# A decoder layer's MLP on one core: turned sums in small buffers, bank copies at other places of a step

## The chip, the cores and the metric

The kernel runs on one core of a Trainium2 chip. The metric is the device time of one execution in microseconds (us); for a program on one core that is the core's own time. The engines that matter here are TensorE (PE in the profile; its weight loads are listed apart as PEld), VectorE (DVE), ScalarE (ACT), GpSimd (POOL, which here only issues DMAs) and SyncE (SP, whose queue carries the loads). Each engine works through its own instructions in order, and semaphores hold an instruction until what it needs is there.

## The reference

One decoder layer on 256 tokens of width 2048, all in float32: an attention branch and a gated convolution branch, merged; an MLP with squared ReLU of width 8192; a gated embedding at the end. The change lies in the MLP and at its border to the last part.

```python
    h = rms_norm(r, g_mlp[i])
    r = r + jnp.square(jax.nn.relu(h @ w_up[i])) @ w_down[i]
    h = rms_norm(r, g_ple[i])
    r = r + jax.nn.sigmoid(h @ w_ple_gate[i]) * (p[i] @ w_ple_proj[i])
```

## The kernel before

**Two parts of every number.** Matmuls take float32 values as a high part, made by ScalarE (`high`, line 135), and a low part, made by VectorE as value minus high part (`low`, line 138). Three matmuls (high by high, high by low, low by high) make one product. So every weight passes ScalarE once and VectorE once before PE uses it.

**Units and items.** The MLP is a loop of 72 steps, `g` = 0 to 71 (line 917). Step `g` has one *unit*: for `g` below 64, 128 columns of `w_up` (result "up"), then eight units of 128 columns of `w_down` ("dn"). PE computes the unit with 15 matmuls of high parts, 16 of low parts and one more (`cols`) into a single PSUM bank; from step 7 on all units share bank 7. ScalarE copies the bank to SBUF (`evacuated`), and the next unit may start in the bank only after this copy.

The other three quarters of `w_down` are multiplied by a Strassen scheme of seven products, in *items* (side, j). An item loads four blocks of weights (`load_pair`), makes sums of them on VectorE, splits all that into high and low parts (`make`, line 717: B11/B22, then B21, then T1/T3, then T2/T4) and, where it is the first item with this j, also the sums of u, S1 to S4 (`sum_u`, split with them). In the step after its `make`, PE multiplies them into seven banks P1 to P7 (`products`, line 776; the order is P1, P3, P5, P7, P2, P6, P4). Most steps have a whole item. Items with j of 24 and more, and two others, are spread over two steps: a *first half-step* (`xs` = 0, 1: B11/B22, the sums of u, T1/T3) and a *second half-step* (`xs` = 2, 3: B21, T2/T4). These are steps 55 to 70.

**Runs and stores.** The seven banks hold the sums of a *run* of items on one side. A run has eight items (the first has four). There are six run ends where the banks have to be given to the other side: `store` (line 793) copies a bank with ScalarE into a tile "part" and issues a DMA on POOL's queue that adds it to DRAM. These 42 copies are queued in `filling`, and `fill()` puts one into ScalarE's order wherever it is called. Before the change all seven are queued at the end of the step in which PE makes the run's last products, so all copies come in the next step: four among the high parts of the next unit and of u, the rest in `make`.

**The stored sums come back.** Late in the loop four `fetch_part` calls (line 807, steps 54, 56, 59 and 61) load stored halves into a tile "raw_p" and queue six jobs each; a step runs two of them behind its bank copy. The first five combine the seven products on ScalarE and VectorE. The last, `turn`, transposes the sums on VectorE into a tile "blocks" and sends them by POOL's queue through DRAM into `r_kept`.

**Buffers.** "slot" is a pool of 44 tiles of 2 KB per partition, from which nearly all small tiles come (u, x, b21, the sums, "part"). Tag "t" has two buffers of 4 KB; "blocks" takes one, and every second item's T2/T4 take two. Tag "raw" has four buffers of 8 KB for weights and "raw_p".

**Order.** From step 2 on `ordered` keeps ScalarE, VectorE, PE and the loads in the order of the program. In one step that order is: `cols` on PE; the parts of the next unit; u of the step before; `make` with the bank's copy in it; two jobs; `products` on PE for the step before. The bank's copy stands behind B11/B22 and the sums of u in a first half-step or a whole step, and behind the high part of T2/T4 in a second half-step (line 766).

**Behind the loop.** In step 71 five of the last inputs x are entered (`enter_high` on ScalarE, `enter_low` on VectorE), P1 is copied twice with a factor each, and sums d and e are made. After the loop come f, c11, the last unit's `dn_done(3, 15)`, the last x, u3, c21, c12 and c22, and PE transposes c11 to c22 between the gate's products.

Of the kernel before, what the change touches and what calls it, by code (L numbers as in the profile page):

```python
# [18 lines left out]
P = 128  # L19
# [19 lines left out]
def hybrid_block_kernel(ctx: ExitStack, tc: tile.TileContext, ins: dict, out: bass.AP):  # L39
# [18 lines left out]
    def slot(shape, dtype, name):  # L58
        return bp.tile(shape, dtype, tag="slot", name=name)
# [75 lines left out]
    def high(hi, src):  # L135
        act(hi, src, AF.Copy)

    def low(lo, src, hi):
        dve.tensor_sub(lo, src, hi.bitcast(F32))
# [577 lines left out]
    def make(a, xs, evacuate):  # L717


        w, j = wS[a], a[1]  # L720
        raw = w["raw"]
        flat = "p a f -> p (a f)"
        fresh = None
        if 0 in xs:
            if j not in sums:
                fresh = sum_u(j)
                sums[j] = tuple(slot([P, 4, P], F32R, f"s_{i}") for i in range(2))
            sh, sl = sums[j]
            for i in range(4):
                w[f"S{i + 1}"] = sh[:, i, :], sl[:, i, :]  # L730
            hi, lo = half_tiles("b")
            keep(w, ("B11", "B22"), hi, lo)
            src = raw[:, 0:2, :].rearrange(flat)
            high(hi, src)
            fill()
            if fresh is not None:
                high(sh, fresh)
            fill()
            low(lo, src, hi)
            fill(len(filling))  # L740
            evacuate()
        if 2 in xs:
            b21 = w["B21"] = tuple(slot([P, CW], F32R, f"b21_{n}") for n in range(2))
            high(b21[0], raw[:, 3, :])
        if 0 in xs:
            dve.tensor_sub(raw[:, 0:3:2, :], raw[:, 0:2, :], raw[:, 2:3, :].to_broadcast([P, 2, CW]))
        if 2 in xs:
            dve.tensor_add(raw[:, 1, :], raw[:, 1, :], raw[:, 0, :])
            low(b21[1], raw[:, 3, :], b21[0])
            dve.tensor_sub(raw[:, 3, :], raw[:, 1, :], raw[:, 3, :])  # L750
        if fresh is not None:
            low(sl, fresh, sh)
        halves = "p (a f) -> p a f"
        if 0 in xs:
            t13 = w["t13"] = half_tiles("t13")
            keep(w, ("T1", "T3"), *t13)
            view = [t.rearrange(halves, a=2) for t in t13]
            high(view[0], raw[:, 0:3:2, :])
            low(view[1], raw[:, 0:3:2, :], view[0])
        if 2 in xs:  # L760
            t24 = half_tiles("t24", items.index(a) % 2 == 0)
            keep(w, ("T2", "T4"), *t24)
            view = [t.rearrange(halves, a=2) for t in t24]
            high(view[0], raw[:, 1:4:2, :])
            if 0 not in xs:
                evacuate()
            low(view[1], raw[:, 1:4:2, :], view[0])


# [37 lines left out]
    def fetch_part(side, h):  # L807
        t = wp.tile([P, 8, S], F32, tag="raw", name="raw_p", bufs=4)
        for i, name in enumerate(ORDER):
            load(t[:, i, :], parts[side, name][:, h * S:(h + 1) * S])  # L810
        p5, p4, p2, p3, p1, p7, p6, z = (t[:, i, :] for i in range(8))
        out = [turned_room(f"turned_s_{side}_{h}_{i}", columns=S) for i in range(2)]

        def first():
            act(z, p1, AF.Copy, scale=up0)
            act(p1, p1, AF.Copy, scale=up1)

        def turn():
            blocks = wp.tile([P, 4, S], F32, tag="t", name="blocks", bufs=2)
            dve.transpose(blocks.rearrange("p a s -> p (a s)"), t[:, 0:4, :].rearrange("p a s -> p (a s)"))  # L820
            for i, half in ((2, 0), (3, 0), (1, 1), (0, 1)):
                nc.gpsimd.dma_start(out[i in (0, 3)][half * P:(half + 1) * P, :], blocks[:, i, :])
            for i in range(2):
                u = 4 * side + 2 * i + h
                st = slot([P, 2, S], F32, "part_in")
                turn_in(st, out[i])
                nc.gpsimd.dma_start(r_kept[u], st, accum_op=ALU.add)

        jobs.extend((
            first,  # L830
            lambda: (scaled(p2, p2, up0, z), scaled(z, p5, down0, z)),
            lambda: (scaled(p3, p3, up0, z), scaled(p7, p7, up1, p1)),
            lambda: (scaled(p7, p6, up1, p7), scaled(p3, p6, up0, p3)),
            lambda: (scaled(p4, p4, down1, p7), scaled(p5, p5, down1, p7)),
            turn,
        ))
# [3 lines left out]
    def fill(n=1):  # L840
        for _ in range(min(n, len(filling))):
            store(*filling.pop(0))
# [74 lines left out]
    for g in range(NU):  # L917
        kind, i = units[g]
        ordered[0] = g > 1
        if g in (5, 7):  # L920
            banks["acc"] = [7, 5] if g == 5 else [7]
        reach = 1 if FIRST <= g < NU - 8 else 2
        for n in range(g + 2, g + reach + 2):
            load_raw(n)
        for a, x in staged[g + 1]:
            if x == 0:
                load_pair(a)
        if g in fetching:
            fetch_part(*fetching[g])
        for u in {NU - 8: (4, 5, 6, 7), NU - 5: (0, 1), NU - 4: (2, 3)}.get(g, ()):  # L930
            load_r(u)
        if g == NU - 3:
            ss2 = slot([P, 2, S], F32, "ss2")
        if g == NU - 2:
            praw = slot([P, 2, S], F32, "p")
            load(praw, ins["pT"].rearrange("p (k s) -> p k s", s=S))
        xs = hT if kind == "up" else {k: uT[16 * i[0] + k] for k in range(16)}
        ps = cols(wU[g][1:], xs, f"{kind}_{g}")
        if g == 0:
            rstd1 = rstd_columns(ss1, "mlp", 1)  # L940
            scales = const.tile([P, 2 * NT], F32, name="scales")
            dve.tensor_mul(scales[:, :NT], rstd1, rstd1)
            dve.tensor_scalar_mul(scales[:, NT:], scales[:, :NT], -1.0)
            up0, up1, down0, down1 = (scales[:, t:t + 1] for t in range(2 * NT))
        if g == 1:
            row1 = rstd_rows(rstd_diag(scales, "mlp"), "mlp")
        done = [n for n in range(g) if n in evac] if g > 1 else []
        ups = [units[n][1] for n in done if units[n][0] == "up"]
        for k in ups:
            up_sum(k, evac.pop(done.pop(0)))  # L950
        halves = []
        while made < g + reach:
            made += 1
            load_raw(made)
            halves += [(made, 0), (made, 1)]
        for h in halves:
            on_act, on_dve = unit_half(*h)
            on_act()
            fill()
            on_dve()  # L960
        for k in ups:
            up_high(k)
        for k in ups:
            up_low(k)
        for n in done:
            dn_done(*units[n][1], evac.pop(n))
        taken = []

        def take():
            if not taken:  # L970
                taken.append(evacuated(ps, kind))

        if staged[g]:
            make(staged[g][0][0], [x for _, x in staged[g]], take)
        fill(len(filling))
        take()
        for _ in range(min(2, len(jobs))):
            jobs.pop(0)()
        entering = {NU - 2: (8, 9), NU - 1: (10, 11, 12, 13, 14)}.get(g, ())
        for n in entering:  # L980
            enter_high(n)
            if n % 2 == 1:
                square(n // 2)
        if g == NU - 1:
            p1 = [evacuated(prod["P1"], "p1", by) for by in (up0, up1)]
        for n in entering:
            enter_low(n)
        if g == NU - 1:
            d, e = (slot([P, CW], F32, n) for n in "de")
            scaled(d, prod["P5"], down0, p1[0])  # L990
            scaled(e, prod["P3"], up0, d)
        evac[g] = taken[0]
        if kind == "up" and i == 63:
            up_sum(i, evac.pop(g))
            up_high(i)
            up_low(i)
        for a, x in staged[g - 1]:
            products(a, x)
            if a in last_of and x == 3:
                filling.extend((a[0], name) for name in NAMES)  # L1000
    assert not jobs


# [36 lines left out]
    f, c11, u3, c12, c21, c22 = (slot([P, CW], F32, n) for n in ("f", "c11", "u3", "c12", "c21", "c22"))  # L1040
    scaled(f, prod["P7"], up1, p1[1])
    scaled(c11, prod["P2"], up0, p1[0])
    dn_done(3, 15, evac.pop(NU - 1))
    enter_high(15)
    square(7)
    scaled(u3, prod["P6"], up1, f)
    scaled(c21, prod["P4"], down1, u3)
    enter_low(15)
    scaled(c12, prod["P6"], up0, e)
    scaled(c22, prod["P5"], down1, u3)  # L1050
# [138 lines left out]
```

## Time and profile before

| | us |
|---|---|
| median of three runs | 1472.6 |
| lowest and highest | 1471.99, 1473.93 |
| profiled execution, its own time | 1475.19 |
| its span, first to last instruction | 1473.4 |
| PE busy | 1428.1 (97%) |
| VectorE busy | 1146.4 (78%) |
| ScalarE busy | 884.2 (60%) |
| POOL busy | 220.7 (15%) |
| mean granted clock of PE | 0.987 |

Shares over the whole span mix stages with different limits. The page's second part, the span in 40 slices, shows where they lie: VectorE is at six or seven tenths up to about 640 us and at nine or more in the MLP's loop; the granted clock is full nearly everywhere, and drops only in stretches from 1200 us on.

The timeline's rows read: start, duration, engine, line, operation, output<-inputs by the program's names, shapes, count, and in brackets how long the engine had been idle before and what released it. Line 87 is the helper for ScalarE, 90 that for PE, 101 that for VectorE, so the names of the tiles tell more than the lines. "w" are the parts of a unit's weights, "raw_s" an item's weights and their sums, "b" those of B11/B22 (wide) or B21 (narrow), "t" those of T1 to T4, "s" those of the sums of u, "a" and "x" u itself, "part" a stored bank, "up" and "dn" the copies of units' banks.

### The profile page before, as it was taken

The numbers are of one execution on the slowest core, as the hardware profiler recorded it, in microseconds if no ns is written. First come the engines' busy times: TensorE is split into PE (matmuls) and PEld (weight loads), VectorE is DVE, ScalarE is ACT, GpSimd is POOL, SyncE is SP. The second block draws the span as 40 slices with busy tenths as digits, with TensorE's granted clock in tenths as the row PEclk, the third lists the DMA queues.
The fourth block names the chain that finished last, engine by engine and source line by source line (L and its number), as shares of the span: only waits on it lengthen the run. The fifth ranks groups of instructions, "written<-read, shape, count | busy, mean of one in ns | idle before, by whom it ended". The sixth has DMA issues, their size and how long they took to land.

```text
span 1473.4 us, 19768 instructions
## 1 busy us (share of the span) xinstructions
PE 1428.1 (97%) x7009; PEld 1198.6 (81%) x7009; DVE 1146.4 (78%) x1718; ACT 884.2 (60%) x1438; POOL 220.7 (15%) x343
## 2 busy tenths in 40 slices
PE   9999999999999999999999999999999987979998
PEld 7888888888888888888787888878888776767888
DVE  7676666666555557759999999999999878888984
ACT  6755545454544444457777777777777655655652
POOL 0043554302020200000100001010000103341000
PEclk9999999999999999999999999999999999989999
DMA  9868777756565666644856769577695857898370
GB/s 280 295 225 265 216 243 238 238 197 219 192 221 200 228 228 222 210 158 154 257 193 210 239 201 251 199 213 237 194 255 173 222 164 222 248 292 237 141 252 22
DMA packets 208371, 318.81 MB, mean 216 GB/s; under 512 B 13840, under 2 KB 134928, under 8 KB 194192
## 3 DMA queue, kind: packets, MB, share of 16 engines
q1 hardware_dynamic: 190272, 280.79, 58.3%
q0 software_dynamic: 17856, 36.72, 10.1%
q8 instruction: 55, 0.90, 0.2%
q14 instruction: 44, 0.36, 0.1%
q10 hardware_dynamic: 144, 0.04, 0.0%
HBM read 290.23 MB, written 26.74 MB: 215 GB/s over the span
## 4 chain that ended last, share of the span: by engine, by line
PE 55%; DVE 18%; issue 17%; DMA 5%; ACT 4%; POOL 1%; SPq 0%; DVEq 0%; ACTq 0%; POOLq 0%
PE ps_g L90 12%; PE ps_o L90 6%; PE ps_pg L90 6%; PE ps_y L90 6%; PE ps_up L90 5%; DVE w_lo L101 4%; DVE raw_s L101 3%; PE ps_k L90 3%; PE ps_q L90 3%; PE ps_cb L90 3%; PE ps_v L90 3%; DVE b_lo L101 2%; DVE t_lo L101 2%; PE P L90 2%; PE ps_cx L90 2%
## 5 line engine op out<-in xcount | busy, mean ns | idle before, releaser
L101 DVE TENSOR_TENSOR w_lo<-raw,w_hi 128x512 fp32r<-128x512 f32 (+1 forms) x524 | 467.9, 927 | 187.6 <-ACT w_hi L87 160.3
L87 ACT ACTIVATE w_hi<-raw 128x512 fp32r<-128x512 f32 (+1 forms) x524 | 406.9, 816 | 257.5 <-PE ps_g L90 63.5
L90 PE MATMUL ps_up<-x,w_hi 128*128 128x512 f32 x1024 | 263.7, 402 | 18.3 <-ACT up L87 18.3
L90 PEld LDWEIGHTS ps_up<-x,w_hi 128*128 128x128 f32 x1024 | 197.0, 194 | 63.2 <-ACT up L87 24.4
L87 ACT ACTIVATE t_hi<-raw_s 128x1024 fp32r<-128x1024 f32 x112 | 118.9, 1062 | 139.6 <-DVE raw_s L101 136.6
L90 PE MATMUL ps_g<-w_hi,x 128*128 128x512 f32 x512 | 158.3, 389 | 0.0
L101 DVE TENSOR_TENSOR raw_s<-raw_s 128x1024 f32<-128x1024 f32 x168 | 146.0, 869 | 5.4
L101 DVE TENSOR_TENSOR t_lo<-raw_s,t_hi 128x1024 fp32r<-128x1024 f32 x112 | 134.8, 1221 | 19.2 <-ACT t_hi L87 16.2
L90 PEld LDWEIGHTS ps_up<-x,w_lo 128*128 128x128 f32 x1024 | 131.3, 191 | 5.0
L90 PE MATMUL ps_up<-x,w_lo 128*128 128x256 f32 x1024 | 132.8, 283 | 0.0
L90 PE MATMUL P<-t_hi,s 128*128 128x512 f32 x336 | 122.8, 393 | 0.0
L90 PEld LDWEIGHTS ps_g<-w_hi,x 128*128 128x128 f32 x512 | 96.1, 188 | 19.9
L798 POOL DMA_DIRECT2D part_P<-part x42 | 32.1, 883 | 487.4 <-ACT part L87 406.8
L90 PE MATMUL ps_g<-w_lo,x 128*128 128x512 f32 x256 | 99.6, 389 | 0.0
L90 PE MATMUL ps_y<-w_hi,x 128*128 128x512 f32 x256 | 79.5, 389 | 0.0
L90 PEld LDWEIGHTS P<-t_hi,s 128*128 128x128 f32 x336 | 63.1, 188 | 15.1 <-ACT part L87 2.6
L101 DVE TENSOR_TENSOR b_lo<-raw_s,b_hi 128x1024 fp32r<-128x1024 f32 x56 | 68.3, 1220 | 3.4 <-ACT b_hi L87 3.4
L90 PE MATMUL ps_pg<-x,w_hi 128*128 128x512 f32 (+1 forms) x272 | 69.7, 389 | 0.0
L87 ACT ACTIVATE a<-a 128x256 f32<-128x256 f32 x128 | 53.1, 415 | 26.6 <-DVE a L101 24.7
L90 PE MATMUL P<-t_lo,s 128*128 128x512 f32 x168 | 65.5, 390 | 1.4 <-DVE t_lo L101 1.4
L87 ACT ACTIVATE b_hi<-raw_s 128x1024 fp32r<-128x1024 f32 x56 | 58.8, 1049 | 5.4 <-DMA raw_s<-in_w_down_dram 3.8
L90 PEld LDWEIGHTS ps_pg<-x,w_hi 128*128 128x128 f32 x272 | 50.6, 193 | 8.4 <-DVE x L101 0.4
(234 smaller groups left out, 2490.8 us busy)
## 6 DMA issues: line engine op xcount, KB each, us to landing
raw<-in_w_up_dram SPq DMA_DIRECT2D x64, 1024.0 KB, 7.3
raw<-in_w_in_dram SPq DMA_DIRECT2D x56, 1024.0 KB, 5.4
raw_s<-in_w_down_dram SPq DMA_DIRECT2D x224, 256.0 KB, 4.0
raw<-in_w_branch_dram SPq DMA_DIRECT2D x16, 1024.0 KB, 5.7
raw<-in_w_o_dram SPq DMA_DIRECT2D x16, 1024.0 KB, 4.9
raw_first<-in_w_qkv_dram SPq DMA_DIRECT2D x48, 256.0 KB, 6.6
raw<-in_w_qkv_dram SPq DMA_DIRECT2D x12, 1024.0 KB, 6.4
part_P<-part POOLq DMA_DIRECT2D x42, 256.0 KB, 10.5
```

Of the source, the lines that this page charges most:

```text
L87: return inorder(nc.scalar.activation(*args, **kw))
L90: return inorder(nc.tensor.matmul(*args, **kw))
L101: return lambda *args, **kw: inorder(getattr(nc.vector, name)(*args, **kw))
L798: nc.gpsimd.dma_start(parts[side, name], st, **how)
```

## The change

Five edits:

- `make` no longer empties the queue of copies ahead of the bank's copy. It calls `fill()` once behind B21's high part, once behind that of T1/T3 and once behind that of T2/T4. In a second half-step the bank is copied behind B21's high part instead of behind that of T2/T4.
- In a step that has a run's last products, these are traced at the step's head (PE's own order is the same), and the seven copies are queued as soon as the bank is copied. So `make` puts three of them (P1, P3, P5) into this step, and four are carried into the next.
- `turn` transposes in two pieces of [128, 2, 256] in tiles of the pool "slot" instead of one of [128, 4, 256] in tag "t".
- In step 71 P1's copies, d and e come ahead of the five x.
- After the loop u3 and c21 come ahead of `dn_done(3, 15)` and the last x.

```diff
             low(lo, src, hi)
-            fill(len(filling))
             evacuate()
         if 2 in xs:
             b21 = w["B21"] = tuple(slot([P, CW], F32R, f"b21_{n}") for n in range(2))
             high(b21[0], raw[:, 3, :])
+            if 0 not in xs:
+                evacuate()
+            fill()
...
             high(view[0], raw[:, 0:3:2, :])
+            fill()
             low(view[1], raw[:, 0:3:2, :], view[0])
...
             high(view[0], raw[:, 1:4:2, :])
-            if 0 not in xs:
-                evacuate()
+            fill()
             low(view[1], raw[:, 1:4:2, :], view[0])
...
-            blocks = wp.tile([P, 4, S], F32, tag="t", name="blocks", bufs=2)
-            dve.transpose(blocks.rearrange("p a s -> p (a s)"), t[:, 0:4, :].rearrange("p a s -> p (a s)"))
-            for i, half in ((2, 0), (3, 0), (1, 1), (0, 1)):
-                nc.gpsimd.dma_start(out[i in (0, 3)][half * P:(half + 1) * P, :], blocks[:, i, :])
+            for i in (2, 0):
+                blocks = slot([P, 2, S], F32, "blocks")
+                dve.transpose(blocks.rearrange("p a s -> p (a s)"), t[:, i:i + 2, :].rearrange("p a s -> p (a s)"))
+                for k in range(2):
+                    half = i == 0
+                    nc.gpsimd.dma_start(out[k != half][half * P:(half + 1) * P, :], blocks[:, k, :])
...
+        ending = any(a in last_of for a, _ in staged[g - 1])
+        carried = len(filling)
+        if ending:
+            assert not filling
+            for a, x in staged[g - 1]:
+                products(a, x)
...
                 taken.append(evacuated(ps, kind))
-
+                if ending:
+                    filling.extend((staged[g - 1][0][0][0], name) for name in NAMES)
+
+        fill(carried)
         if staged[g]:
             make(staged[g][0][0], [x for _, x in staged[g]], take)
-        fill(len(filling))
         take()
         for _ in range(min(2, len(jobs))):
             jobs.pop(0)()
+        if g == NU - 1:
+            p1 = [evacuated(prod["P1"], "p1", by) for by in (up0, up1)]
+            d, e = (slot([P, CW], F32, n) for n in "de")
+            scaled(d, prod["P5"], down0, p1[0])
+            scaled(e, prod["P3"], up0, d)
...
-        if g == NU - 1:
-            p1 = [evacuated(prod["P1"], "p1", by) for by in (up0, up1)]
         for n in entering:
             enter_low(n)
-        if g == NU - 1:
-            d, e = (slot([P, CW], F32, n) for n in "de")
-            scaled(d, prod["P5"], down0, p1[0])
-            scaled(e, prod["P3"], up0, d)
...
-        for a, x in staged[g - 1]:
-            products(a, x)
-            if a in last_of and x == 3:
-                filling.extend((a[0], name) for name in NAMES)
+        if not ending:
+            for a, x in staged[g - 1]:
+                products(a, x)
...
     scaled(c11, prod["P2"], up0, p1[0])
+    scaled(u3, prod["P6"], up1, f)
+    scaled(c21, prod["P4"], down1, u3)
     dn_done(3, 15, evac.pop(NU - 1))
     enter_high(15)
     square(7)
-    scaled(u3, prod["P6"], up1, f)
-    scaled(c21, prod["P4"], down1, u3)
     enter_low(15)
```

## The prediction

> **What bounds the kernel now.** I read the page first (TensorE, PE below, is busy for 97% of the span), then busy times by run of eight items, then one run engine by engine, then the waits of the loop's last 160 us. The change touches only the loop of 72 steps (about 640 to 1358 us) and what follows it directly. Times are us from the span's start.
>
> One run of eight items, from one run's end to the next (stretch: its length, then busy time of PE, PE's weight loads, VectorE, ScalarE, POOL, then granted clock, DMA share, GB/s):
>
> ```profile
> 719.67:804.57 84.90, 83.75 (x426) 70.48 (x425) 82.47 (x110) 62.66 (x92) 3.81 (x7) 1.00 0.67 221
> ```
>
> PE and VectorE are both nearly full, so the question is which of them sets the 84.90. PE, from its timeline, and its waits for the store copies in the whole loop (total, times, longest):
>
> ```profile
> 726.80 3.57 PE L90 MATMUL ps_up<-x,w_hi 128*128 128x512 f32 x15
> ...
> 737.13 3.56 PE L90 MATMUL ps_up<-x,w_hi 128*128 128x512 f32 x15
> ```
>
> ```profile
> PE P L90 <- ACT part L87: 6.5, 11, 0.8
> ```
>
> An undisturbed PE step is 737.13 - 726.80 = 10.33, eight are 82.64. PE has 84.90 - 82.64 = 2.26 of slack in a run, and spends it at the run's end, waiting for store copies and filling up again. VectorE:
>
> ```profile
> 723.17 0.29 DVE L101 TENSOR_TENSOR x_first<-a,x_first 128x128 fp32r<-128x128 f32 x1 [0.81 <-ACT x_first L87]
> 724.11 1.23 DVE L101 TENSOR_TENSOR b_lo<-raw_s,b_hi 128x1024 fp32r<-128x1024 f32 x1 [0.66 <-ACT b_hi L87]
> ```
>
> These are its only waits in the run: 82.47 busy, 1.47 waiting and 0.96 between 110 instructions make 84.90. **VectorE is the chain**, and PE's store stalls are slack. So I price the change by VectorE's gaps, and look at PE only to see that it doesn't become the bound.
>
> **The change part by part.**
>
> *Three copies earlier.* ScalarE at that run's end:
>
> ```profile
> 715.37 1.06 ACT L87 ACTIVATE t_hi<-raw_s 128x1024 fp32r<-128x1024 f32 x1 [1.73 <-DVE raw_s L101]
> 717.43 1.07 ACT L87 ACTIVATE t_hi<-raw_s 128x1024 fp32r<-128x1024 f32 x1 [0.99 <-DVE raw_s L101]
> 718.39 1.04 ACT L87 ACTIVATE w_hi<-raw 128x1024 fp32r<-128x1024 f32 x1
> 719.34 0.58 ACT L87 ACTIVATE part<-P 128x512 f32<-128x512 f32 x1
> 719.82 1.05 ACT L87 ACTIVATE w_hi<-raw 128x1024 fp32r<-128x1024 f32 x1
> ...
> 723.01 1.07 ACT L87 ACTIVATE b_hi<-raw_s 128x1024 fp32r<-128x1024 f32 x1
> ```
>
> From 717.43 to b_hi ScalarE never idles, with four copies in between, and that makes VectorE's two gaps. A copy takes 0.48 of its time (719.34 to 719.82). After the change P1's copy falls into the 1.73 and P3's into the 0.99; P5's stands behind the last t_hi, and the other four where four stand now. So b_hi comes one copy later: 0.48 at each of six run ends, **+2.9**. Ends: 0 if ScalarE finds room elsewhere, +5.7 if P3's copy shows too. The added wait, of ScalarE on P1's last product with t_hi queued behind, is short: P1's three products are PE's first behind the unit's bank, which ScalarE has copied just before. PE's stalls go, which is worth nothing while VectorE is the chain. Three DMA issues of line 798 move a step forward on POOL's queue, which has next to nothing else to do in a run (3.81 of 84.90 busy).
>
> *What that does to buffers.* The stores' source tiles come from the pool from which b21 is taken:
>
> ```profile
> 1073.21 0.69 DVE L101 TENSOR_TENSOR b<-raw_s,b 128x512 fp32r<-128x512 f32 x1 [1.67 <-DMA part_P<-part]
> ...
> 1164.03 0.69 DVE L101 TENSOR_TENSOR b<-raw_s,b 128x512 fp32r<-128x512 f32 x1 [5.60 <-DMA part_P<-part]
> ```
>
> At the fifth and sixth run end VectorE waits for a store to land, the first or second of its run, in whose tile b21 is to lie. P1's copy now starts at 715.37 less the idle 1.73, 5.7 before its 719.34, and P3's some 4 before its place, about the longer wait. I take **-1.67 and -5.60**; ends 0 and that.
>
> *Turn in small buffers.* VectorE's waits for high parts from 1195 to 1352 (total, times, longest), then two rows of its timeline:
>
> ```profile
> DVE t_lo L101 <- ACT t_hi L87: 12.8, 15, 1.2
> ```
>
> ```profile
> 1215.71 1.25 DVE L101 STREAM_TRANSPOSE blocks<-raw_p 128x1024 f32<-128x1024 f32 x1 [9.15 <-PE P L90]
> ...
> 1253.89 1.23 DVE L101 TENSOR_TENSOR t_lo<-raw_s,t_hi 128x1024 fp32r<-128x1024 f32 x1 [2.96 <-DMA turned_s<-blocks]
> ```
>
> The first transpose waits for a tag "t" buffer, which holds T2 and T4 until PE has used them a step later; at the second turn T2 and T4 wait for the buffer that the blocks hold. With buffers of their own the first wait goes, **-9.15**, and of the second what exceeds the 1.2 that t_lo has anyway, **-1.8**. Ends: 0 each, should the new buffers not be free either. VectorE's next waits there are those 1.2. The transposes (count | busy, mean ns):
>
> ```profile
> L101 DVE STREAM_TRANSPOSE blocks<-raw_p 128x1024 f32<-128x1024 f32 x4 | 5.0, 1245 | 9.4 <-PE P L90 9.2
> ...
> L101 DVE STREAM_TRANSPOSE blocks<-q 128x512 f32<-128x512 f32 x4 | 2.6, 686 | 0.0
> ```
>
> Two of 686 ns for one of 1245, four times: **+0.5**. A turn's four POOL DMAs keep their bytes; only the order of two changes.
>
> *Unit banks ahead of the last high part.* PE in half-steps, then two rows of VectorE:
>
> ```profile
> 1205.05 6.41 PE L90 MATMUL ps_up<-x,w_hi 128*128 128x512 f32 x15 [3.40 <-ACT up L87]
> ...
> 1222.00 6.46 PE L90 MATMUL ps_up<-x,w_hi 128*128 128x512 f32 x15 [6.11 <-ACT up L87]
> 1228.30 2.08 PE L90 MATMUL ps_up<-x,w_lo 128*128 128x256 f32 x16
> 1230.22 0.40 PE L90 MATMUL ps_up<-x,w_hi 128*128 128x512 f32 x1
> ...
> 1316.28 5.30 PE L90 MATMUL ps_dn<-x,w_hi 128*128 128x512 f32 x15 [2.25 <-ACT dn L87]
> ```
>
> ```profile
> 1230.64 0.69 DVE L101 TENSOR_TENSOR raw_s<-raw_s 128x512 f32<-128x512 f32 x1
> ...
> 1325.35 1.23 DVE L101 TENSOR_TENSOR t_lo<-raw_s,t_hi 128x1024 fp32r<-128x1024 f32 x1 [1.06 <-ACT t_hi L87]
> ```
>
> In a second half-step the bank's copy stands behind t_hi, and t_hi behind VectorE: PE waits 3.40 and then runs 15 matmuls in 6.41 instead of 3.56. With the copy behind b21's high part that stall goes. But in a first half-step the bank's copy still follows the high part of the sums of u, which VectorE gates, so PE will wait there instead, and VectorE still sets the pair. What is new is t_hi behind a copy that waits for PE. Behind the 1222.00 (slow clock) the unit ends at 1230.62, VectorE's sum for t_hi at 1231.33: 0.7 to spare, so t_hi isn't held up. At 1325.35 t_lo lost half a us against the 0.5 usual in a first half-step, because PE's bank was late after the slow 5.30; this goes: **-0.5**. Ends 0 and -2.
>
> [...]
>
> *The loop's end.* VectorE, then PE:
>
> ```profile
> 1357.52 0.88 DVE L101 SCALAR_TENSOR_TENSOR x<-r,vec,x 128x256 fp32r<-128x256 f32 x2 [1.05 <-ACT x L87]
> 1358.83 0.89 DVE L101 SCALAR_TENSOR_TENSOR x<-r,vec,x 128x256 fp32r<-128x256 f32 x2 [0.43 <-ACT x L87]
> 1360.15 0.48 DVE L101 SCALAR_TENSOR_TENSOR x<-r,vec,x 128x256 fp32r<-128x256 f32 x1 [0.43 <-ACT x L87]
> 1360.72 0.75 DVE L101 SCALAR_TENSOR_TENSOR d<-P,scales,p 128x512 f32<-128x512 f32 x1
> ```
>
> ```profile
> 1365.49 0.58 PE L90 MATMUL ps_pg<-x,w_lo 128*128 128x256 f32 x1 [1.29 <-ACT x L87]
> ```
>
> PE waits for the last x (1365.49), and after it for nothing more. u3 and c21 ahead of that x cost it 2 x 0.75 = 1.5. For it, d and e move into the 1.05 + 0.43 + 0.43 = 1.9 in which VectorE waits for x. That alone is -0.4; c21 ready earlier spares PE's transposes, which wait for it too, about as much again: **-0.8**. Ends +1.5 (d and e cover nothing) and -2.
>
> **Sum**: 2.9 - 1.67 - 5.60 - 9.15 - 1.8 + 0.5 - 0.5 - 0.8 = -16.1. The profiled execution took 1475.19 (span 1473.4), which makes 1459.1. The median of the runs, 1472.6, lies 2.6 below it; carried over: **1456.5**.
>
> **The rivals.**
>
> *PE is the bound in the runs.* Then its six losses count, 6 x 2.26 = 13.6, and the extra copy is hidden: 1456.5 - 13.6 - 2.9 = 1440.0, or about 1448 if half of it holds. Against it: VectorE's run adds up without a gap. 0.07.
>
> *Loads come late.* Busy time, ScalarE and VectorE behind the 1300:
>
> ```profile
> 1300.00:1310.00 10.00, 10.00 (x56) 8.70 (x55) 9.22 (x15) 5.77 (x7) 2.01 (x4) 1.00 1.07 359
> ```
>
> ```profile
> 1300.69 1.06 ACT L87 ACTIVATE b_hi<-raw_s 128x1024 fp32r<-128x1024 f32 x1 [2.62 <-DMA raw_s<-in_w_down_dram]
> ```
>
> ```profile
> 1302.58 1.22 DVE L101 TENSOR_TENSOR b_lo<-raw_s,b_hi 128x1024 fp32r<-128x1024 f32 x1
> ```
>
> The DMA engines are full, and VectorE had 1302.58 - 1301.75 = 0.8 to spare. With the steps closer together some five pairs lose 1 to 2 each: 1462 to 1466. Against it: VectorE's own progress frees the buffers, so the loads move with it. 0.15.
>
> *PE's clock drops twice a pair.* Start to start of two PE half-steps, and the sums of u, one pair apart:
>
> ```profile
> 1232.96 3.68 PE L90 MATMUL ps_up<-x,w_hi 128*128 128x512 f32 x15
> ...
> 1240.91 3.56 PE L90 MATMUL ps_up<-x,w_hi 128*128 128x512 f32 x15
> ```
>
> ```profile
> L101 DVE TENSOR_TENSOR s_raw<-a,s_raw x2: 282/283/284, 1220.5 to 1239.0; 128x128 f32<-128x128 f32 x2
> ```
>
> PE takes 2 x 7.95 = 15.9 for a pair, one drop 2.9 more (6.46 - 3.56), 18.8 at most, of which the gap before it is part of VectorE's 18.5 (1239.0 - 1220.5). With a second drop, 21.7, it is 3.2 over, on some four pairs: 1456.5 + 13 = 1469.5. Against it: the second drop needs a second long stall, and its place is gone. 0.05.
>
> *Slower: the turn's new buffers are not free.* They come from the pool in which VectorE waited 5.60. POOL's longest wait for a turn's DMA:
>
> ```profile
> 1285.84 4.04 POOL L420 DMA_DIRECT2D part_in<-turned_s  x6 [7.63 <-DMA turned_s<-blocks]
> ```
>
> If VectorE must wait for such a DMA at each of four turns, up to 4 x 7.63 = 30.5 come on top: 1487. It decides from 16.1 / 4 = 4.0 a turn. Against it: from 1195 to 1352 VectorE waits for no buffer of that pool. 0.04.
>
> *The change doesn't do what it says*: b21 and the transposes get their buffers as late as before. Then 2.9 + 0.5 - 0.5 - 0.8 = 2.1 is left: 1474.7. 0.05.
>
> **How the numbers follow.** Forecast 0.64. With its terms halfway to their ends it reaches about 8 to either side. 1448 to 1466 holds the forecast (0.61), late loads (0.14) and part of the first rival (0.05). Faster by over 0.2% (2.9 us, about what a measurement of this kernel can tell from no change): 0.64 + 0.07 + 0.15 + 0.05 = 0.91; within it 0.04; slower 0.05, the last two rivals shared out.
>
> **What would show it.** Right: no wait of VectorE on a store's or a turn's DMA, nor of the blocks on PE; its two gaps at a run's start 1.95 together instead of 1.47; PE's waits on "part" gone and a run still at about 85; PE's stalls in half-steps of 2 to 4, now in front of the unit that follows a first half-step. Wrong: a run of 83 (PE was the bound); ScalarE's high parts waiting for loads; VectorE waiting for the blocks.

## The result, and the profile after

| us | before | after |
|---|---|---|
| median of the runs made together (4 each) | 1472.3 | 1452.09 |
| lowest and highest | 1470.67, 1473.93 | 1450.9, 1453.02 |
| profiled execution, own time | 1475.19 | 1451.77 |
| its span | 1473.4 | 1450.0 |

After over before is 0.9862, 95% interval 0.9845 to 0.9879: 20 us faster. The forecast was 1456.5, with 1448 to 1466 as its range, so it holds the time, and the sign and most terms came out. But the time is 4.4 below the forecast, and the question is where that went.

First what the prediction said one would see. A run of eight items, measured at the same point of the order as before (stretch, length, then busy time of PE, its weight loads, VectorE, ScalarE, POOL; clock; DMA share; GB/s):

```profile
719.00:804.34 85.34, 83.81 (x427) 70.59 (x426) 82.50 (x110) 62.66 (x92) 3.78 (x8) 1.00 0.68 221
```

It was 84.90 and is 85.34, although PE no longer waits for a store copy in the loop. VectorE's timeline at the run's start, after:

```profile
720.69 1.22 DVE L101 TENSOR_TENSOR w_lo<-raw,w_hi 128x1024 fp32r<-128x1024 f32 x1 [0.17 <-ACT w_hi L87]
...
722.96 0.29 DVE L101 TENSOR_TENSOR x_first<-a,x_first 128x128 fp32r<-128x128 f32 x1 [1.04 <-ACT x_first L87]
723.91 1.23 DVE L101 TENSOR_TENSOR b_lo<-raw_s,b_hi 128x1024 fp32r<-128x1024 f32 x1 [0.66 <-ACT b_hi L87]
```

The gaps are 0.17 + 1.04 + 0.66 = 1.87 where 1.47 stood: the extra copy ahead of b_hi. VectorE's waits from 1190 to 1352 after (total, times, longest), all that are left there:

```profile
DVE t_lo L101 <- ACT t_hi L87: 13.4, 16, 1.2
DVE x L101 <- ACT x L87: 2.0, 2, 1.4
DVE w_lo L101 <- ACT w_hi L87: 1.1, 3, 0.5
DVE b_lo L101 <- ACT b_hi L87: 0.2, 1, 0.2
```

No wait for the blocks, for a store or for a turn's DMA is among them. PE's stalls in the half-steps, after:

```profile
1207.36 5.30 PE L90 MATMUL ps_up<-x,w_hi 128*128 128x512 f32 x15 [3.30 <-ACT up L87]
1226.20 3.69 PE L90 MATMUL ps_up<-x,w_hi 128*128 128x512 f32 x15 [1.05 <-ACT up L87]
1244.94 5.29 PE L90 MATMUL ps_up<-x,w_hi 128*128 128x512 f32 x15 [2.32 <-ACT up L87]
1264.51 5.32 PE L90 MATMUL ps_dn<-x,w_hi 128*128 128x512 f32 x15 [1.78 <-ACT up L87]
1275.76 3.70 PE L90 MATMUL ps_dn<-x,w_hi 128*128 128x512 f32 x15 [1.27 <-ACT dn L87]
1287.71 6.30 PE L90 MATMUL ps_dn<-x,w_hi 128*128 128x512 f32 x15 [3.82 <-ACT dn L87]
```

They stand in front of the unit that follows a first half-step, as foretold, but are 1.05 to 3.82 long where 2 to 4 was said; no stall is left behind a second half-step.

Then the terms. VectorE's b_lo, t_lo and x are the same instructions in both kernels, and so is the one behind each turn's transposes. The change of the distance of their starts, from one to the next, prices each edit. The table is worked out from their rows in both traces:

| term | predicted | between the traces |
|---|---|---|
| ahead of the loop's runs (no edit there) | 0 | -0.7 |
| copy ahead of b_hi, six run ends | +2.9 | +2.9 |
| b21's tile, fifth and sixth run end | -1.67, -5.60 | -1.8, -5.7 |
| blocks of the first turn | -9.15 | -9.2 |
| T2/T4 of the second turn | -1.8 | -1.8 |
| transposes split | +0.5 | -0.3 |
| loads that come late behind the first and third turn | 0 | +0.5 |
| bank's copy in second half-steps, up to the last t_lo | -0.5 | -1.2 |
| last t_lo to the last x | -0.8, with the next | -2.3 |
| last x to the span's end | | -3.7 |
| small drifts and rounding | | -0.1 |
| sum | -16.1 | -23.4 |

All terms inside the loop stand within 0.8. Two of them need a word. The split transposes are busy for longer, about 1.30 against 1.25 a turn, but from the job before them to the instruction behind them VectorE took 2.07, 2.15 and 2.15 at the last three turns and takes 2.01 at each: the split gains a little. What is lost behind the first turn, 0.4, is a load. ScalarE's and VectorE's timeline, after:

```profile
1211.35 2.01 ACT L87 ACTIVATE w_hi<-raw 128x1024 fp32r<-128x1024 f32 x2 [0.76 <-DMA raw<-in_w_up_dram]
```

```profile
1212.44 2.36 DVE L101 TENSOR_TENSOR w_lo<-raw,w_hi 128x1024 fp32r<-128x1024 f32 x2 [0.29 <-ACT w_hi L87]
```

In a second execution of the changed kernel (the run "once more" below) VectorE's t_lo stand 8.14 apart there, as before; here they stand 8.52 apart. Why the load was late, no run shows.

The loop's end gave 5.9 instead of 0.8. These rows show it. Of before, the windows view, then VectorE's and PE's timeline:

```profile
1360.00:1370.00 10.00, 6.03 (x24) 4.52 (x24) 9.49 (x16) 4.48 (x9) 0.00 (x0) 0.73 0.00 0
```

```profile
1350.10 1.23 DVE L101 TENSOR_TENSOR t_lo<-raw_s,t_hi 128x1024 fp32r<-128x1024 f32 x1 [1.21 <-ACT t_hi L87]
```

```profile
1350.60 3.70 PE L90 MATMUL ps_dn<-x,w_hi 128*128 128x512 f32 x15 [0.60 <-ACT dn L87]
...
1358.57 1.70 PE L90 MATMUL ps_pg<-x,w_hi 128*128 128x512 f32 x6
...
1363.79 0.41 PE L535 MATMUL tr<-ident,c 128*128 128x128 f32 x2 [2.69 <-DVE c L101]
...
1456.61 3.57 PE L90 MATMUL ps_pg<-x,w_hi 128*128 128x512 f32 x15
```

And the same views and instructions after:

```profile
1340.00:1350.00 10.00, 8.15 (x42) 6.13 (x43) 9.25 (x17) 4.11 (x9) 0.00 (x0) 1.00 0.01 5
```

```profile
1332.61 1.22 DVE L101 TENSOR_TENSOR t_lo<-raw_s,t_hi 128x1024 fp32r<-128x1024 f32 x1 [1.19 <-ACT t_hi L87]
```

```profile
1330.63 3.56 PE L90 MATMUL ps_dn<-x,w_hi 128*128 128x512 f32 x15
...
1338.46 0.61 PE L90 MATMUL ps_pg<-x,w_hi 128*128 128x512 f32 x2
1340.39 1.69 PE L90 MATMUL ps_pg<-x,w_hi 128*128 128x512 f32 x4 [1.32 <-DVE x L101]
...
1343.30 0.44 PE L535 MATMUL tr<-ident,c 128*128 128x128 f32 x2 [0.38 <-DVE c L101]
1344.81 0.87 PE L535 MATMUL tr<-ident,c 128*128 128x128 f32 x6 [1.08 <-DVE c L101]
...
1433.19 3.57 PE L90 MATMUL ps_pg<-x,w_hi 128*128 128x512 f32 x15
```

Two things are to be seen. The last unit began 0.50 behind the step's t_lo and now begins 1.98 ahead of it. And PE's way from its first gate product to the same late one was 1456.61 - 1358.57 = 98.04 and is 94.73. Its waits on it were 2.69 + 1.29 = 3.98 (the second is a row of the prediction) and are 1.32 + 0.38 + 1.08 = 2.78; that is 1.2 of the 3.3 by which the way is shorter. The rest goes with the granted clock, 0.73 before and 1.00 after.

### The profile page after: what moved, and what is told of

It is laid out like the page before. It is cut to its first block, busy times and chain, and to the rows that moved or that the text cites. A ratio compares the mean times of both kernels' runs of the same rounds, so it can differ in the third digit from the quotient of the medians.

```text
span 1450.0 us, 19774 instructions
## 1 busy us (share of the span) xinstructions
PE 1420.0 (98%) x7009; PEld 1194.6 (82%) x7009; DVE 1144.8 (79%) x1722; ACT 884.8 (61%) x1438; POOL 220.4 (15%) x343
## 3 DMA queue, kind: packets, MB, share of 16 engines
q0 software_dynamic: 17856, 36.72, 10.3%
## 4 chain that ended last, share of the span: by engine, by line
PE 58%; DVE 26%; issue 7%; ACT 6%; DMA 2%; POOL 0%; SPq 0%; DVEq 0%; ACTq 0%; POOLq 0%
PE ps_g L90 12%; PE ps_o L90 7%; PE ps_pg L90 6%; PE ps_y L90 6%; DVE w_lo L101 6%; DVE raw_s L101 5%; DVE b_lo L101 4%; DVE t_lo L101 4%; PE ps_up L90 3%; PE ps_q L90 3%; PE ps_k L90 3%; PE ps_cx L90 3%; PE ps_cb L90 3%; PE ps_cc L90 3%; PE ps_v L90 3%
## 5 line engine op out<-in xcount | busy, mean ns | idle before, releaser
L90 PE MATMUL ps_up<-x,w_hi 128*128 128x512 f32 x1024 | 260.1, 397 | 15.1 <-ACT up L87 15.1
L90 PEld LDWEIGHTS ps_up<-x,w_hi 128*128 128x128 f32 x1024 | 192.3, 190 | 63.5 <-ACT up L87 26.4
```

The source lines that it names most:

```text
L90: return inorder(nc.tensor.matmul(*args, **kw))
```

## The experiments

All times are medians of 4 to 12 runs. Ratios are to runs of the kernel before on the same chip, whose median was 1471.45 beside the first four, 1472.49 beside the next four and 1470.53 beside the last four.

### One part of the change at a time

*The turn alone.*

```diff
-            blocks = wp.tile([P, 4, S], F32, tag="t", name="blocks", bufs=2)
...
+                blocks = slot([P, 2, S], F32, "blocks")
```

> The kernel before, with the turn's edit alone (two transposes of 128x512 in tiles of the pool slot). VectorE is the chain (forecast): its 9.15 for the blocks goes, and of the T2/T4 wait 1.8, the split transposes cost 0.5: -10.5, and up to -14 if the loop's end, reached earlier, also loses its slow-clock stretch; VectorE's waits for a store's DMA (1.67 and 5.60) stay. Rival, the new tiles wait for the pool: the 9.15 comes back as a wait on a DMA in front of the new transposes and the time is within 2 of the kernel before.

1462.04, ratio 0.9937 (0.9922 to 0.9952), which on 1471.45 is -9.3 (-7.1 to -11.5). VectorE's waits from 640 to 1190 still have the longer of the two on a store (the shorter did not show in this execution):

```profile
DVE b L101 <- DMA part_P<-part: 4.9, 1, 4.9
```

The forecast's term holds; the new tiles wait for nothing.

*The store copies alone*, with the bank's copy of the second half-steps kept late:

```diff
+        if ending:
+            for a, x in staged[g - 1]:
+                products(a, x)
...
+                if ending:
+                    filling.extend((staged[g - 1][0][0][0], name) for name in NAMES)
```

> The kernel before, with only the store copies moved (three banks of a run copied in the step of its last block, the products traced at the step's head); the bank's copy of a second half-step stays behind the high part of T2/T4. VectorE is the chain (forecast): -1.67 - 5.60 + 2.9 = -4.4, a run stays at about 85.3 between its ends, and PE's waits on part are gone all the same. Rival, PE is the bound in the runs: its 2.26 of a run come back too, six times 2.26 and 7.3 = -21, and a run is 82.6 to 83.

1468.45, ratio 0.9984 (0.9974 to 0.9994): -2.4 (-0.9 to -3.8). A run takes 85.35 between its ends, and PE's waits on "part" are gone. That is short of the 4.4 of the chain, which lies outside the interval, and far from the 21 of the rival. In the traces the loop itself gives the forecast's term: from its first b_lo to its last t_lo this run takes 681.35 and the kernel before 685.55, 4.2 more. **PE's store stalls were slack.**

*The bank's copy alone.*

```diff
             high(b21[0], raw[:, 3, :])
+            if 0 not in xs:
+                evacuate()
```

> The kernel before, with only the bank's copy of the second half-steps moved behind B21's high part. VectorE sets the pair (forecast): -0.5 to -1 by the last x, PE's stalls of 3.40, 6.11 and so on are found in front of the unit that follows a first half-step instead, of 2 to 4; if PE's shorter wait at the loop's end also keeps the clock there, up to -4. Rival, each stall of PE in a second half-step is lost time: some 15 of stalls and with their slow stretches up to 24 go.

1462.96, ratio 0.9944 (0.993 to 0.9958): -8.2 (-6.2 to -10.3). That was neither of the two. VectorE's timeline of this run at the first turn, and its t_lo of the last step with PE's last unit:

```profile
1206.27 1.25 DVE L101 STREAM_TRANSPOSE blocks<-raw_p 128x1024 f32<-128x1024 f32 x1 [2.77 <-PE P L90]
...
1339.08 1.23 DVE L101 TENSOR_TENSOR t_lo<-raw_s,t_hi 128x1024 fp32r<-128x1024 f32 x1 [1.19 <-ACT t_hi L87]
```

```profile
1337.08 3.56 PE L90 MATMUL ps_dn<-x,w_hi 128*128 128x512 f32 x15
```

The wait for the blocks fell from 9.15 to 2.77 with nothing done to the turn: PE, without its stall in the half-step before, had used T2 and T4 6.4 earlier. This gain and 6.4 of the turn's are one and the same, so the parts taken alone count it twice. The four of them add up to -23.0 (9.3 + 2.4 + 8.2 + 3.1), and the change gave -20.3 (0.0138 of 1471.45); with intervals of about 2 on each part, these sums alone would not show it. And the last unit begins 2.00 ahead of t_lo, as in the changed kernel, so the last x comes 2.6 earlier behind t_lo. That part is not in the term.

*The loop's end alone.*

```diff
+    scaled(u3, prod["P6"], up1, f)
+    scaled(c21, prod["P4"], down1, u3)
     dn_done(3, 15, evac.pop(NU - 1))
```

(and P1's copies, d and e ahead of the five x)

> The kernel before, with only the order at the loop's end changed (P1's copies, d and e ahead of the five x of the last step; u3 and c21 ahead of the last unit's sum). By the forecast's term -0.8. The two traces show more: 2.3 by the last x and 5.9 to the span's end between the kernels, with the granted clock down to 0.73 behind the loop before and at full speed after. If the order alone does this: -4 to -6, and PE's waits of 2.69 and 1.29 ahead of the last x's product are below 1.5 each with the clock at 1.0. Rival, PE's earlier arrival at the loop's end does it (the other edits): -0.8 to -2 and the clock still drops between 1360 and 1380.

1468.46, ratio 0.9979 (0.9967 to 0.9991): -3.1 (-1.3 to -4.9). From the last x to the span's end it has 103.39, before 107.07, after 103.42. PE's timeline and the window of these waits:

```profile
1356.45 1.73 PE L90 MATMUL ps_pg<-x,w_hi 128*128 128x512 f32 x4 [0.50 <-DVE x L101]
...
1359.92 0.44 PE L535 MATMUL tr<-ident,c 128*128 128x128 f32 x2 [0.91 <-DVE c L101]
1361.44 0.88 PE L535 MATMUL tr<-ident,c 128*128 128x128 f32 x6 [1.07 <-DVE c L101]
```

```profile
1353.00:1363.00 10.00, 7.52 (x36) 5.36 (x36) 7.76 (x15) 5.11 (x11) 0.00 (x0) 1.00 0.18 61
```

In this execution the order alone does it: three short waits, full clock. The median gives a little less than the 4 to 6 expected. In the run of the bank's copy alone, PE came as early as in the changed kernel, and the clock still fell (windows view of that run):

```profile
1350.00:1360.00 10.00, 8.83 (x36) 7.00 (x37) 9.83 (x17) 6.13 (x11) 0.00 (x0) 0.68 0.00 0
```

So PE's earlier arrival, the rival, does not keep the clock.

### The loop's end, undone in parts

The changed kernel with the whole order put back; with only u3 and c21 put back; with only P1's copies, d and e put back (diffs against the changed kernel are the lines above the other way round).

> The changed kernel with the loop's end in the order of the kernel before. By the forecast's term the order is worth 0.8: 1452.9. By the run of the loop's end alone it is worth 3.6 (the last x is 0.1 later, and what follows it 3.7 shorter because PE's clock stays at 1.0): 1455 to 1456, and the clock drops to about 0.7 in the ten us behind the last unit again.

> The changed kernel with u3 and c21 behind the last unit's sum again, and P1's copies, d and e still ahead of the five x. If PE's wait for c21 is what stops the clock (forecast's second half of the loop's end): PE waits about 2 to 3 at once for c21, the clock drops, and it is 2 to 3.5 slower than the changed kernel. If the order of d and e does it: within 0.5 of the changed kernel.

> The changed kernel with the five x ahead of P1's copies, d and e again, and u3 and c21 still ahead of the last unit's sum. VectorE has the same work up to c21, and PE waits for c21 either way: within 0.5 of the changed kernel, with one wait of some 1.7 for c11 in place of 1.32 and 0.38. If the order of d and e is what keeps the clock: 2 to 3.5 slower than the changed kernel.

1455.11 (ratio 0.9884, 0.9871 to 0.9898), 1453.25 (0.9875, 0.9859 to 0.9892) and 1453.63 (0.9872, 0.9859 to 0.9886). The whole order is worth about 3, which is the expectation from the run alone and not the 0.8. The halves are worth a us or two each; the intervals do not tell them from the changed kernel or from each other. In the profiles the clock fell in all three. One row of the windows view of each, in that order:

```profile
1345.00:1355.00 10.00, 9.11 (x41) 7.54 (x42) 9.67 (x16) 6.74 (x11) 0.00 (x0) 0.71 0.08 14
```

```profile
1345.00:1355.00 10.00, 7.90 (x35) 6.18 (x35) 9.83 (x17) 5.55 (x10) 0.00 (x0) 0.83 0.00 1
```

```profile
1345.00:1355.00 10.00, 10.00 (x48) 8.62 (x47) 9.39 (x17) 6.74 (x11) 0.00 (x0) 0.78 0.10 23
```

So in these executions neither half alone kept the clock, which goes against both one-sided expectations. The waits differ from the expected ones too: with u3 and c21 put back no wait of PE there is longer than 1.35, where 2 to 3 for c21 was expected, and with d and e put back the one for c11 is 2.20 and not 1.7. The profiled execution of the second version is the slowest of its four, 1456.43; the others took 1452.66 to 1453.57. How far one execution can be taken for the rule, the last section shows.

### The bank's copy, undone

Beside the changed kernel once more: its bank's copy late in all second half-steps, and late in all but the last.

```diff
-            if 0 not in xs:
+            if 0 not in xs and a == items[-1]:
                 evacuate()
```

> The changed kernel once more, beside the next three runs. 1451 to 1453; whether the clock drops behind the last unit may differ from execution to execution, which moves it by about 2.

> The changed kernel with the bank's copy of a second half-step behind the high part of T2/T4 again. By the forecast's term the earlier copy is worth 0.5: 1452.6. By the run of the bank copy alone it is worth 1.1 in the half-steps and 2.6 at the last unit, which starts 2.5 earlier and which VectorE waits for: 3.7 slower, 1455 to 1457, the last unit of w_down again begins after t_lo of the step before, and VectorE waits 1.9 for the last inputs x.

> The changed kernel with the earlier bank's copy in the last half-step alone, and behind the high part of T2/T4 in all the others. If the gain of this edit is made at the last unit: 2.6 of the 3.7 stay, so within 0.5 to 1.5 of the changed kernel, although PE's stalls of 2 to 6 are back in the second half-steps. Rival, these stalls cost by themselves: as slow as with the copy late everywhere, 1455 to 1457.

1451.41 (ratio 0.9867, 0.9847 to 0.9886), 1457.09 (0.9902, 0.9886 to 0.9919) and 1455.68 (0.9894, 0.9875 to 0.9913). Undoing it everywhere costs 5.7. Between the two profiles it is 4.7: 0.8 ahead of step 55 (0.7 of it ahead of the loop's first b_lo, where nothing was edited), 1.5 in the half-steps from there on and 2.4 between the last t_lo and the last x. Without the 0.8 that is 3.9, where 3.7 was expected. Of the 1.9 expected as waits for the last x, 1.0 is seen; another 1.2 is a wait for P1's copy. Keeping the copy early in the last half-step alone did **not** keep the gain, against my expectation: by the medians 4.3 are lost. Its four runs spread from 1453.82 to 1457.97, and the profiled one is the slowest. Its trace shows where that execution lost time. PE, ScalarE and VectorE around 1240, and PE's last unit:

```profile
1238.74 6.57 PE L90 MATMUL ps_up<-x,w_hi 128*128 128x512 f32 x15 [3.33 <-ACT up L87]
...
1335.71 3.56 PE L90 MATMUL ps_dn<-x,w_hi 128*128 128x512 f32 x15
```

```profile
1247.48 0.60 ACT L87 ACTIVATE up<-ps_up 128x512 f32<-128x512 f32 x1 [2.57 <-PE ps_up L90]
1247.98 1.05 ACT L87 ACTIVATE t_hi<-raw_s 128x1024 fp32r<-128x1024 f32 x1
```

```profile
1249.06 1.22 DVE L101 TENSOR_TENSOR t_lo<-raw_s,t_hi 128x1024 fp32r<-128x1024 f32 x1 [1.82 <-ACT t_hi L87]
...
1335.95 1.23 DVE L101 TENSOR_TENSOR t_lo<-raw_s,t_hi 128x1024 fp32r<-128x1024 f32 x1 [1.19 <-ACT t_hi L87]
```

PE stalls in the second half-step, runs slow behind it (6.57), and its unit ends late; in the first half-step the unit's copy stands ahead of t_hi, and VectorE waits 1.82 where 0.53 is usual. That is the mechanism of the forecast's -0.5, only longer. Part of it goes with the execution: with the copy late everywhere PE had the same wait of 3.33 in front of this unit, but its 15 matmuls took 5.13 and not 6.57, and t_lo waited the usual 0.53. And PE still enters the last steps late: its last unit begins 0.24 ahead of t_lo, not 1.98. So a stall that VectorE hides for several steps can come out where VectorE has nothing more to split; how much of the 4.3 that is, these runs do not show.

### The carried copies behind b_hi

If VectorE is the chain of a run, its 1.87 at the run's start are to be had: the carried copies ahead of b_hi make them. Here all four stand behind b_hi, and none among the next unit's and u's high parts.

```diff
             high(hi, src)
-            fill()
+            fill(len(filling))
...
-        fill(carried)
```

> The changed kernel with the four carried store copies put behind the high part of B11/B22 (they stand ahead of it, among the next unit's and u's high parts). VectorE is the chain (forecast): its gaps of 1.87 at each run's start fall to 0.3, six times 1.6 = 9.4, so 1442 to 1444, a run takes 83.5 to 84, and PE's waits on part or on up take back 1 at most. Rival, PE is now the bound in the runs: no gain, or slower, because the banks P7, P2, P6 and P4 and the unit's bank come free 2 later; a run stays at 85.3 and PE's waits on part are back.

1443.66, ratio 0.98 (0.9784 to 0.9817). The same stretch of the run, and VectorE and ScalarE at its start:

```profile
718.46:802.18 83.72, 82.41 (x422) 70.31 (x421) 82.38 (x109) 62.89 (x92) 3.77 (x8) 1.00 0.69 222
```

```profile
722.08 1.23 DVE L101 TENSOR_TENSOR b_lo<-raw_s,b_hi 128x1024 fp32r<-128x1024 f32 x1 [0.38 <-ACT b_hi L87]
```

```profile
721.01 1.04 ACT L87 ACTIVATE b_hi<-raw_s 128x1024 fp32r<-128x1024 f32 x1
721.96 2.04 ACT L87 ACTIVATE part<-P 128x512 f32<-128x512 f32 x4
```

A run takes 83.72 instead of 85.34, and b_lo moves ahead by about 1.65 at each of the six run ends, 9.9 in all. PE waits on "part" again (4.8 in total) and it costs nothing. This is the test that the forecast's first step lacked: **VectorE's gap was the price of a run**. By the last t_lo the profile is 9.8 ahead of the changed kernel's; 8.0 are left at the span's end, since the clock fell behind the loop in this execution (to 0.79 from 1335 to 1345; 105.22 from the last x to the end, not 103.42). It beats both kernels.

*d and e last.* On that version, d and e put behind the last unit's sum, and c11 ahead of f:

```diff
+    scaled(c11, prod["P2"], up0, p1[0])
     scaled(f, prod["P7"], up1, p1[1])
-    scaled(c11, prod["P2"], up0, p1[0])
...
+    scaled(d, prod["P5"], down0, p1[0])
     enter_low(15)
+    scaled(e, prod["P3"], up0, d)
```

> The version with the four carried store copies behind the high part of B11/B22, and with d and e, which only c12 needs, moved behind the last unit's sum, c11 ahead of f. Behind the last unit PE is the bound: its waits of 1.32 for x and 0.3 for c11 go and that for c21 stays at about 1.2, and the clock no longer drops there, so 1.6 to 3 below the run without this, 1440 to 1442, with less spread. Rival, VectorE is the bound there (it has the same work): no change, 1443 to 1444.

1443.0, ratio 0.9808 (0.979 to 0.9825): no difference. VectorE now waits for x itself, and PE for c21:

```profile
1332.10 0.88 DVE L101 SCALAR_TENSOR_TENSOR x<-r,vec,x 128x256 fp32r<-128x256 f32 x2 [0.43 <-ACT x L87]
1333.40 0.48 DVE L101 SCALAR_TENSOR_TENSOR x<-r,vec,x 128x256 fp32r<-128x256 f32 x1 [0.43 <-ACT x L87]
```

```profile
1336.97 0.87 PE L535 MATMUL tr<-ident,c 128*128 128x128 f32 x6 [1.38 <-DVE c L101]
```

d and e had covered those 0.43, as the prediction meant them to. In front of c21, VectorE or ScalarE's x is the bound whatever comes first, so the rival held. The mean clock of all four runs is 0.995 or 0.996, where three of the five runs without this edit had 0.993; that the order did this is not shown.

## Why the prediction was right, and where not

- *VectorE is the chain of a run*: right. The copy ahead of b_hi cost 0.49 at each run end (+2.9), PE's store stalls went for nothing, and putting the carried copies behind b_hi gave 1.65 a run. The sum that the prediction drew it from closes by construction, since the 0.96 between the instructions is what was left over; it is the runs with the copies moved that show it. Late in the loop, from about 1140 us, the page of before has VectorE at seven or eight tenths and not at nine: there lie most of the waits that the change takes away.
- *The buffers* (-1.67, -5.60, -9.15, -1.8): right within 0.1 each. The split's +0.5 was added up from busy times; between starts the split gains 0.3. And the 9.15 was not the turn's alone: it is a wait for PE to let go of T2 and T4, and the bank's earlier copy by itself takes 6.4 of it. Taken alone, the parts count it twice.
- *Unit banks ahead of the last high part, -0.5*: mis-sized. "VectorE still sets the pair" holds up to step 70. Step 71 has no item to make, and there PE's place counts: the last unit begins 2.5 earlier against t_lo. With that the term is -3.5 between the traces (1.2 + 2.3), and by the medians undoing it costs 5.7.
- *The loop's end, -0.8*: the step that failed. It priced VectorE's instructions up to the last x and gave PE's transposes "about as much again". Measured, the order brings the last x no earlier (0.1 later when made alone, 0.4 later beside the other edits) and shortens what follows it by 3.7 and 3.2. From c21 on PE is the bound, and its waits of 2.69 and 1.29 cost their own length and a slow stretch behind them (granted clock 0.73 from 1360 to 1370). The prediction quoted the 1.29 and the slow clock of other stretches, but did not look at the clock of this one.
- *Rivals*: PE as the bound of a run fell with the copies alone and with the copies behind b_hi. A second clock drop in a pair and new buffers that are not free did not show: none of VectorE's waits from 1190 on is on a DMA or a buffer. That a drop needs a long stall, as the case against the first of these had it, did not hold: behind a wait of 1.78 the clock was 0.68 in one execution. Late loads did show, in small: they reached VectorE through ScalarE's high parts and cost 0.5 in the profiled execution, not the 5 to 10 of that rival.
- *The median*: the terms fell 7.3 short (23.4 less 16.1), the forecast only 4.4. The 2.6 by which the profiled execution of before lay over its median were carried over, and that hid part of the error: the profiled execution of after lies 0.3 below its median.

## What to carry to other kernels

Ask at each border of a stage which engine sets the time behind it: a stall that costs nothing while another engine is the chain is paid where that engine runs out of work. When two edits remove the same wait from two sides, it is to be counted once. And a copy that another engine waits for goes ahead of copies that only free a buffer.

## What the runs showed of the hardware

*Short idle times of PE can be followed by a lower clock.* In the changed kernel's first profile 15 matmuls mostly took 3.56 without a wait. Behind waits of 1.05 and 1.27 they took 3.69 and 3.70, with the granted clock still at 1.00. Behind 1.78 and 2.32 they took 5.32 and 5.29, as behind 3.30 (5.30), each time at a clock of 0.68; behind 3.82 they took 6.30 at 0.55.

*The same wait may or may not do it.* In the changed kernel, run once more, the unit that had waited 1.78 waits 1.74, and its 15 matmuls take 3.71, as those that ran at 1.00 above:

```profile
1264.19 3.71 PE L90 MATMUL ps_dn<-x,w_hi 128*128 128x512 f32 x15 [1.74 <-ACT up L87]
```

That run and the version with the copies behind b_hi also have the same wait of 1.32 behind the last unit. PE's timeline and the windows view of the first:

```profile
1339.82 1.69 PE L90 MATMUL ps_pg<-x,w_hi 128*128 128x512 f32 x4 [1.32 <-DVE x L101]
```

```profile
1345.00:1355.00 10.00, 10.00 (x62) 8.48 (x60) 9.41 (x16) 7.05 (x12) 0.00 (x0) 1.00 0.14 31
```

and of the second:

```profile
1330.58 1.68 PE L90 MATMUL ps_pg<-x,w_hi 128*128 128x512 f32 x4 [1.32 <-DVE x L101]
```

```profile
1335.00:1345.00 10.00, 10.00 (x48) 8.72 (x49) 9.35 (x17) 6.74 (x11) 0.00 (x0) 0.79 0.05 15
```

The waits that follow within 5 us are shorter in the second (0.82, against 0.39 and 1.07 in the first), and yet its clock fell. The versions with the bank's copy late, everywhere or in all but the last half-step, are another such pair: PE's waits behind the last unit are 0.49, 0.91 and 1.08 in the one and 0.49, 0.92 and 1.08 in the other, and from the last x to the span's end they take 103.41 at full clock and 104.80 with the clock down (1.00 and 0.83 from 1345 to 1355). So with the new order at the loop's end the clock stayed full in most profiles and not in all. All five profiles without any of it (the kernel before, the three other parts alone, the changed kernel with the order undone) lost the clock there (0.66 to 0.73 in a stretch of 10 us) and took 106.5 to 107.1 from the last x on. Of the six profiles with the whole new order, four kept it (1.00; 103.4), and two lost part of it (0.83 and 0.79; 104.80 and 105.22).

The five runs of the copies behind b_hi fall into two groups: 1441.18 and 1441.57 with a mean clock of 0.996, and 1443.66 to 1444.98 with 0.993. So some 2 to 3 us of these kernels' spread go with the clock; that each of them lies at the loop's end was seen in one profile only. Why the clock falls behind a wait in one execution and not behind the same wait in another, no run here shows.
